# A two-layer kernel on one core: five buffers for weights, the index lookup by halves, gates that end five blocks earlier

## The chip, the core and the metric

One NeuronCore of a Trainium2 chip runs the whole program in one launch. The metric is device time in microseconds. Three runs of the kernel before took 2858.58, 2861.81 and 2862.98 us; the median is 2861.81.

TensorE (PE in the profile) multiplies matrices, VectorE (DVE) and ScalarE (ACT) work elementwise, GpSimd (POOL) issues the indirect gathers, and SyncE (SP) issues most of the other transfers. ACT issues some too.

## The reference

Two layers are computed on one sequence of 1024-wide tokens. Each layer is a mixer (A: gated linear attention and attention to a memory; B: stick-breaking attention) and a PEER step, each closed by a residual and a layer norm. PEER is where most of the time goes:

```
q        = x @ wq                              # 8 heads, two half queries each
s1, s2   = scores of the half queries against two sets of 128 subkeys
top16 of s1, top16 of s2 -> 256 sums -> top16  # per head
expert   = 128 * i1 + i2                       # 16384 experts
g        = softmax(best 16 scores)
y[t]     = sum over heads, experts of  g * gelu(x[t] . u[expert]) * v[expert]
x        = layer_norm(ALPHA * x + y)
```

All products are wanted in nearly fp32 precision.

## The kernel before, in words

**Tokens.** The first token tile (128 tokens) and 16 side tokens go by gather: for each chosen expert, POOL fetches a row of `un` or `vt`, and DVE multiplies and sums it (`gr` L1156, `va` L1175). The other tokens, 368 per chunk, go densely: all 16384 rows of u are multiplied with x, the result goes through gelu and is multiplied with a matrix of gates that is zero where an expert isn't chosen, and then comes the product with v.

**Blocks.** A PEER step runs 16 query blocks, 128 u blocks and 128 v blocks. A block of u is a 512 KB tile `ur` of raw weights, loaded by SP (L82). ACT rounds it (`uh`, L97), DVE subtracts to get the rest (`ul`, L98), and PE makes 24 matmuls of 128x368: eight chunks times `uh`·`xhi` (L117), `uh`·`xlo` (L118) and `ul`·`xhi` (L119). A v block has `vr`, `vh`, `vl` and 18 matmuls of 512 columns (L285, L287, L289) that accumulate into `acc`. The raw tiles have RB = 4 buffers and the split ones 3. In iteration b of the u loop the split of block b + 2 is made, so `ul` of block b + 2 stands on DVE behind all that iteration b puts there.

**Side work.** The same loop carries DVE's other work in small pieces, as Python generators that yield an estimate in ns. `work(...)` runs the top-k, the index lookup, the softmax and `gate_prep` of the next token tiles up to a budget per block (WB = 1000 once a tile is ready, WB0 = 1700 ahead of that). `gst(GR)` builds one-hots (`ob` L1462, `ob`·`gT` L1468, side tokens L1438) and has PE multiply them into gates (`pg` L1511), GR = 1.25 steps per block; `gus` handles the gathered rows with a budget of GU = 1230, and GU2 = 1350 or GU3 = 1900 once `work` is empty. The engines take their instructions in the order in which this program issues them.

**Index lookup** (L1283 to L1302). For four heads at a time, the 16 places in two lists are turned into indices: ACT spreads the list (`tb`), DVE compares the places with 0 to 15 (`eq` L1292, 128x1024), multiplies (L1296) and adds up in four steps (L1300, L1302). The two lists ("halves") have buffers of their own and go side by side, operation by operation.

**Gates.** ACT writes the gates to DRAM (`Gd`, L1516). When the last are written, SP loads the gates of the first v blocks into a tile that the profile calls `keep` (L1665, `keep<-Gd`), and ACT's queue issues the next two loads (`gl`). For a v block DVE and ACT multiply gates with activations into `w` (L1700, L1702), and ACT and DVE split it (`whi` L1704, `wlo` L1705).

**End of a PEER step.** The last TAIL = 5 v blocks are done tile by tile for each 128 tokens, and after each tile comes its layer norm (`lny` L984, `lnst` L985, and so on to L1001) while PE is at the next tile. After the last tile nothing covers the layer norm but the next mixer, or nothing at all at the end of the kernel.

Of the kernel before, what the change touches and what calls it, by code (L numbers as in the profile page):

```python
# [408 lines left out]
def mixer_a(E, a):  # L409
# [4 lines left out]
    with tc.tile_pool(name="acat", bufs=1, reuse_waits="tile") as ap:  # L414
# [11 lines left out]
        with psum_pool(E, acc=4, ps=4), tc.tile_pool(name="mixwk", bufs=2, reuse_waits="tile") as wk, \  # L426
# [4 lines left out]
            w2 = mp.tile([16, 3, P], F32, name="w2")  # L431
# [184 lines left out]
            with tc.manual_schedule(engines={mybir.EngineType.PE}):  # L616
# [8 lines left out]
                aT = [mp.tile([P, NT, P], F32, name=f"aT{h}") for h in range(GH)]  # L625
# [348 lines left out]
def layer_norm(E, lp, t, halves, gam, bet, hooks=()):  # L974
# [3 lines left out]
    y = lp.tile([P, D], F32, tag="lny", name="lny")  # L978
# [54 lines left out]
WB, WB0 = 1000, 1700  # L1033
# [7 lines left out]
GU2 = 1350  # L1041
GU3 = 1900
# [10 lines left out]
def peer(E, mixer, wq, sk, ut, vt, un, lng, lnb, out_dram=None, follow=()):  # L1053
# [10 lines left out]
    with ExitStack() as pp:  # L1064
# [118 lines left out]
        with ExitStack() as up:  # L1183
# [21 lines left out]
            class Sel:  # L1205
# [48 lines left out]
                def indices(self, h0=0, h1=8):  # L1254
# [28 lines left out]
                    for h in range(0, h1 - h0, ih):  # L1283
                        hs = slice(h, h + ih)
                        tb, eq = [], []
                        for half in range(2):
                            tb.append(wk.tile([P, 4, 16, 16], F16, tag=f"tb{half}", name="tb", bufs=1)[:, :ih])
                            nc.scalar.activation(tb[half], tv[:, half, hs, :, None].to_broadcast([P, ih, 16, 16]), AF.Copy)
                        for half in range(2):
                            eq.append(wk.tile([P, 4, 16, 16], F16, tag=f"eq{half}", name="eq", bufs=1)[:, :ih])  # L1290
                            av = ab[:, half, :n].rearrange("p (h k) -> p h k", k=16)
                            nc.vector.tensor_tensor(eq[half], av[:, hs, None, :].to_broadcast([P, ih, 16, 16]),  # L1292
                                                    E.iota16[:, None].to_broadcast([P, ih, 16, 16]), op=ALU.is_equal)
                        yield 300 * ih
                        for half in range(2):
                            nc.vector.tensor_mul(eq[half], eq[half], tb[half])  # L1296
                        yield 300 * ih
                        for m in (8, 4, 2):
                            for e in eq:
                                nc.vector.tensor_add(e[:, :, 0:m], e[:, :, 0:m], e[:, :, m:2 * m])  # L1300
                        for half, e in enumerate(eq):
                            nc.vector.tensor_add(self.i12[:, half, h0 + h:h0 + h + ih], e[:, :, 0], e[:, :, 1])  # L1302
                        yield 500 * ih
# [535 lines left out]
```

## Time and profile before

| | |
|---|---|
| median of three runs | 2861.81 us |
| the profiled execution, its own time | 2858.78 us |
| its span | 2857.1 us |
| PE busy | 2829.1 us |
| DVE busy | 2410.4 us |
| ACT busy | 1445.3 us |
| POOL busy | 778.2 us |
| mean DMA rate | 282 GB/s |

In the profiled execution layer 1's u blocks run from 335.65 to 901 us and its v blocks to about 1410 us; layer 2's u blocks run from 1754.47 to 2319.8 us. Rows of the timeline give start and duration in us, engine, line of the kernel, operation and tiles; in brackets stands how long the engine had been idle just before, and what ended that. A row with x2 or more has several instructions together.

### The profile page before, as it was taken

The numbers are of one execution on the slowest core, as the hardware profiler recorded it, in microseconds if no ns is written. First come the engines' busy times: TensorE is split into PE (matmuls) and PEld (weight loads), VectorE is DVE, ScalarE is ACT, GpSimd is POOL, SyncE is SP. The second block draws the span as 40 slices with busy tenths as digits, with TensorE's granted clock in tenths as the row PEclk, the third lists the DMA queues.
The fourth block names the chain that finished last, engine by engine and source line by source line (L and its number), as shares of the span: only waits on it lengthen the run. The fifth ranks groups of instructions, "written<-read, shape, count | busy, mean of one in ns | idle before, by whom it ended". The sixth has DMA issues, their size and how long they took to land. (4 is left out here: it accounts for less than half of the span.)

```text
span 2857.1 us, 44575 instructions
## 1 busy us (share of the span) xinstructions
PE 2829.1 (99%) x16144; PEld 2507.4 (88%) x16144; DVE 2410.4 (84%) x4944; ACT 1445.3 (51%) x2723; POOL 778.2 (27%) x584
## 2 busy tenths in 40 slices
PE   9999999999999999999999999999999999999998
PEld 7888899999998888888877789999999988888886
DVE  5567999999877888888868779999998778888888
ACT  6342446757674333433446424477676744334333
POOL 0100253333333333333000002433333333234330
PEclk9999999999999999999999999999999999999999
DMA  5332589989999999999521325989999999999994
GB/s 194 103 112 67 176 313 321 343 316 342 340 344 369 338 371 370 373 380 365 195 81 52 111 82 202 327 319 325 327 343 342 340 368 336 373 375 371 368 359 165
DMA packets 311070, 806.87 MB, mean 282 GB/s; under 512 B 32176, under 2 KB 124480, under 8 KB 304448
## 3 DMA queue, kind: packets, MB, share of 16 engines
q1 hardware_dynamic: 195936, 414.93, 42.0%
q0 software_dynamic: 78336, 285.25, 27.6%
q10 hardware_dynamic: 36576, 103.85, 9.5%
q8 instruction: 126, 2.06, 0.3%
q14 instruction: 96, 0.79, 0.1%
HBM read 708.19 MB, written 94.68 MB: 281 GB/s over the span
## 5 line engine op out<-in xcount | busy, mean ns | idle before, releaser
L117 PE MATMUL ph<-xhi,uh 128*128 128x368 f32 x2048 | 687.7, 336 | 0.0
L119 PE MATMUL ph<-xhi,ul 128*128 128x368 f32 x2048 | 674.0, 329 | 1.2 <-DVE ul L98 1.2
L118 PE MATMUL ph<-xlo,uh 128*128 128x368 f32 x2048 | 673.4, 329 | 0.0
L1103 POOL DMA_INDIRECT gr<-in_un,gidx x256 | 392.8, 1534 | 796.9 <-DVE gr L1156 595.3
L97 ACT ACTIVATE vh<-vr 128x1024 fp32r<-128x1024 f32 x256 | 271.3, 1060 | 497.7 <-PE acc L289 445.2
L1103 POOL DMA_INDIRECT gr<-in_vt,gidx x256 | 311.8, 1218 | 646.9 <-DVE va L1175 553.4
L285 PE MATMUL acc<-vh,whi 128*128 128x512 f32 x1536 | 474.5, 390 | 4.5 <-ACT whi L1704 4.5
L287 PE MATMUL acc<-vl,whi 128*128 128x512 f32 x1536 | 474.2, 390 | 0.2
L289 PE MATMUL acc<-vh,wlo 128*128 128x512 f32 x1536 | 473.6, 389 | 0.0
L98 DVE TENSOR_TENSOR vl<-vr,vh 128x1024 fp32r<-128x1024 f32 x256 | 313.5, 1225 | 160.1 <-ACT vh L97 156.6
L97 ACT ACTIVATE uh<-ur 128x1024 fp32r<-128x1024 f32 x288 | 304.1, 1056 | 197.9 <-PE ph L118 174.3
L119 PEld LDWEIGHTS ph<-xhi,ul 128*128 128x128 f32 x2048 | 384.7, 188 | 2.2 <-DVE ul L98 2.2
L118 PEld LDWEIGHTS ph<-xlo,uh 128*128 128x128 f32 x2048 | 385.4, 188 | 0.0
L117 PEld LDWEIGHTS ph<-xhi,uh 128*128 128x128 f32 x2048 | 385.1, 188 | 0.1
L98 DVE TENSOR_TENSOR ul<-ur,uh 128x1024 fp32r<-128x1024 f32 x288 | 351.1, 1220 | 34.3 <-ACT uh L97 34.3
L285 PEld LDWEIGHTS acc<-vh,whi 128*128 128x128 f32 x1536 | 287.9, 188 | 66.4 <-ACT whi L1704 7.0
L287 PEld LDWEIGHTS acc<-vl,whi 128*128 128x128 f32 x1536 | 288.3, 188 | 61.7 <-DVE vl L98 2.2
L289 PEld LDWEIGHTS acc<-vh,wlo 128*128 128x128 f32 x1536 | 288.2, 188 | 60.8 <-DVE wlo L1705 1.0
L1156 DVE SCALAR_TENSOR_TENSOR gr<-gr,xnat 128x1024 f32<-128x1024 f32 x256 | 310.3, 1218 | 24.5 <-DMA gr<-in_un,gidx 24.5
L1175 DVE SCALAR_TENSOR_TENSOR va<-gr,gw,va 128x1024 f32<-128x1024 f32 x254 | 325.2, 1281 | 1.0
L1491 ACT ACTIVATE obl<-ob,rat 128x128 f16<-128x128 f16 x736 | 234.1, 392 | 38.0 <-DVE ob L1468 18.3
L1704 ACT ACTIVATE whi<-w 128x384 fp32r<-128x384 f32 x256 | 131.1, 512 | 78.5 <-DVE w L1700 78.1
(358 smaller groups left out, 4091.4 us busy)
## 6 DMA issues: line engine op xcount, KB each, us to landing
ur<-in_ut SPq DMA_DIRECT2D x256, 512.0 KB
vr<-in_vt SPq DMA_DIRECT2D x256, 512.0 KB
Gd<-gt ACTq DMA_DIRECT2D x48, 1024.0 KB
Ad<-act ACTq DMA_DIRECT2D x112, 368.0 KB
al<-Ad SPq DMA_DIRECT2D x112, 368.0 KB
gl<-Gd SPq DMA_DIRECT2D x26, 1536.0 KB
ur<-in_wq SPq DMA_DIRECT2D x32, 512.0 KB
bs<-in_b_st SPq DMA_DIRECT2D x14, 512.0 KB
```

The source lines that it names most:

```text
L97: nc.scalar.activation(hi, raw, AF.Copy)
L98: sub = lambda: eng.tensor_sub(lo, raw, hi.bitcast(F32))
L117: nc.tensor.matmul(ps, h, xhi[:, c, sl], start=(c == 0), stop=False)
L118: nc.tensor.matmul(ps, h, xlo[:, c, sl], start=False, stop=False)
L119: nc.tensor.matmul(ps, l, xhi[:, c, sl], start=False, stop=(c == NC - 1))
L285: nc.tensor.matmul(acc[hf], lh, hi[:, hf * 512:(hf + 1) * 512], start=first, stop=False)
L287: nc.tensor.matmul(acc[hf], lh, lo[:, hf * 512:(hf + 1) * 512], start=False, stop=False)
L289: nc.tensor.matmul(acc[hf], ll, hi[:, hf * 512:(hf + 1) * 512], start=False, stop=last)
L1103: nc.gpsimd.indirect_dma_start(out=gr, out_offset=None, in_=tab, in_offset=bass.IndirectOffsetOnAxis(ap=idx[:, k:k + 1], axis=0))
L1156: nc.vector.scalar_tensor_tensor(gr, gr, 1.0, xr, op0=ALU.mult, op1=ALU.mult, accum_out=dst[:, k:k + 1])
L1175: nc.vector.scalar_tensor_tensor(va, gr, gw[:, k:k + 1], va, op0=ALU.mult, op1=ALU.add)
L1491: nc.scalar.activation(obl[:, q], ob[:, q, 0], AF.Copy, scale=rat[:, n0 + q:n0 + q + 1])
```

## The change

It has seven parts.

1. RB goes from 4 to 5; `w2` shares a buffer with `aT0`, `lny` has one buffer in place of two, and `tb` and `eq` have one each in place of two.
2. The index lookup goes half by half: all six operations of one half, then all of the other. ACT spreads the next half once DVE has multiplied the last one.
3. WB0 goes from 1700 to 1850; GU2 and GU3 become 1550 both; the gate builder makes 1.4 steps per block (GR2) once the `work` queue is empty; `work` falls to its small budget also where side gates are ready and more than one builder waits.
4. `gate_prep` yields after `ghi` and is told as 1000 + 1900 in place of 2500; the stream of the tiles yields 2000 in place of 4000 before the last one.
5. The gates end five blocks earlier, so the first load of gates and the first `w` move from the turn into the u blocks; the third load of gates is issued at v block 6 in place of 1.
6. The activation that loads the square-root table comes 8 v blocks later.
7. The last dense tile's tail runs by halves of 512 columns: first all 15 matmuls of the first half, then those of the second.

```diff
-WB, WB0 = 1000, 1700
+WB, WB0 = 1000, 1850
-GU2 = 1350
-GU3 = 1900
+GU2 = 1550
+GU3 = 1550
+GR2 = 1.4
-RB = 4
+RB = 5
...
-                    for h in range(0, h1 - h0, ih):
...
-                        yield 300 * ih
-                        for half in range(2):
-                            nc.vector.tensor_mul(eq[half], eq[half], tb[half])
-                        yield 300 * ih
-                        for m in (8, 4, 2):
-                            for e in eq:
-                                nc.vector.tensor_add(e[:, :, 0:m], e[:, :, 0:m], e[:, :, m:2 * m])
-                        for half, e in enumerate(eq):
-                            nc.vector.tensor_add(self.i12[:, half, h0 + h:h0 + h + ih], e[:, :, 0], e[:, :, 1])
-                        yield 500 * ih
+                    tb = spread(*todo[0])
+                    for k, (h, half) in enumerate(todo):
+                        eq = wk.tile([P, 4, 16, 16], F16, tag="eq", name="eq", bufs=1)[:, :ih]
...
+                        yield 150 * ih
+                        nc.vector.tensor_mul(eq, eq, tb)
+                        if k + 1 < len(todo):
+                            tb = spread(*todo[k + 1])
                         for m in (8, 4, 2):
+                            nc.vector.tensor_add(eq[:, :, 0:m], eq[:, :, 0:m], eq[:, :, m:2 * m])
+                        nc.vector.tensor_add(self.i12[:, half, h0 + h:h0 + h + ih], eq[:, :, 0], eq[:, :, 1])
+                        yield 400 * ih
...
                     nc.vector.tensor_copy(ghi, h16)
+                    yield 1000
...
-                    yield 2500
+                    yield 1900
...
-                yield 4000
+                yield 2000
                 yield from prev.gate_prep()
...
-                gst(GR)
+                gst(GR if work.q else GR2)
...
-                    work(WB if ready else WB0)
+                    work(WB if ready or sready and len(gst.q) > 1 else WB0)
...
-                if b == 1:
+                if b == 6:
                     preload(2)
...
                 if b == P // 2:
                     vp["ln"] = load_ln(E, wv, lng, lnb)
+                if b == P // 2 + 8:
                     warm_sqrt(E, vp["ln"][0])
...
+                if t < ND - 1:
+                    for k, (whi, wlo, hi, lo) in enumerate(tail):
+                        mov_mm(E, acc[t], whi[:, sl], wlo[:, sl], hi, lo, False, k == TAIL - 1)
+                else:
+                    for hf in range(2):
+                        hs = slice(hf * 512, (hf + 1) * 512)
+                        for k, (whi, wlo, hi, lo) in enumerate(tail):
+                            nc.tensor.matmul(acc[t][hf], whi[:, sl], hi[:, hs], start=False, stop=False)
+                            nc.tensor.matmul(acc[t][hf], whi[:, sl], lo[:, hs], start=False, stop=False)
+                            nc.tensor.matmul(acc[t][hf], wlo[:, sl], hi[:, hs], start=False, stop=k == TAIL - 1)
```

DVE's order before at u blocks 7 to 9 of layer 1, from the comparison behind `ul` of block 6 to `ul` of block 9 (`gr` is the product with a gathered row):

```order
L1292 TENSOR_TENSOR eq<-ab,iota_65 128x1024 x2
L1156 SCALAR_TENSOR_TENSOR gr,gh<-gr,xnat 128x1024
L98 TENSOR_TENSOR ul<-ur,uh 128x1024
L1296 TENSOR_TENSOR eq<-eq,tb 128x1024 x2
L1156 SCALAR_TENSOR_TENSOR gr,gh<-gr,xnat 128x1024
L98 TENSOR_TENSOR ul<-ur,uh 128x1024
L1300 TENSOR_TENSOR eq<-eq 128x4x128 x2
L1300 TENSOR_TENSOR eq<-eq 128x4x64 x2
L1300 TENSOR_TENSOR eq<-eq 128x4x32 x2
L1302 TENSOR_TENSOR i_2258<-eq 128x64 x2
L1156 SCALAR_TENSOR_TENSOR gr,gh<-gr,xnat 128x1024
L98 TENSOR_TENSOR ul<-ur,uh 128x1024
```

And in the changed kernel, the block of the first half, from the comparison to `ul` of block 7:

```order
L1295 TENSOR_TENSOR eq<-ab,iota_65 128x1024
L1298 TENSOR_TENSOR eq<-eq,tb 128x1024
L1302 TENSOR_TENSOR eq<-eq 128x4x128
L1302 TENSOR_TENSOR eq<-eq 128x4x64
L1302 TENSOR_TENSOR eq<-eq 128x4x32
L1303 TENSOR_TENSOR i_2258<-eq 128x64
L1157 SCALAR_TENSOR_TENSOR gr,gh<-gr,xnat 128x1024
L98 TENSOR_TENSOR ul<-ur,uh 128x1024
```

The pair took three blocks, each operation twice in a row; a half takes one block with all its six operations, and the other half follows in the next block in the same way.

At the turn from u to v, DVE's order before, from the gathered rows at the last `ul` of layer 1 (the first `w` belongs to v block 0):

```order
L98 TENSOR_TENSOR ul<-ur,uh 128x1024
L1156 SCALAR_TENSOR_TENSOR gr,gh<-gr,xnat 128x1024 x3
L1700 TENSOR_TENSOR w<-keep 128x368
L98 TENSOR_TENSOR vl<-vr,vh 128x1024
L1705 TENSOR_TENSOR wlo<-w,whi 128x384
```

And in the changed kernel, from the first `w` on:

```order
L1702 TENSOR_TENSOR w<-keep 128x368
L98 TENSOR_TENSOR ul<-ur,uh 128x1024
L1157 SCALAR_TENSOR_TENSOR gr,gh<-gr,xnat 128x1024 x2
L98 TENSOR_TENSOR ul<-ur,uh 128x1024
L1157 SCALAR_TENSOR_TENSOR gr,gh<-gr,xnat 128x1024
L98 TENSOR_TENSOR ul<-ur,uh 128x1024
L1157 SCALAR_TENSOR_TENSOR gr,gh<-gr,xnat 128x1024
L98 TENSOR_TENSOR ul<-ur,uh 128x1024
L1157 SCALAR_TENSOR_TENSOR gr,gh<-gr,xnat 128x1024
L98 TENSOR_TENSOR ul<-ur,uh 128x1024
```

The first `w` stood behind the last `ul`; now six `ul` (the sixth stands two rows further on) come after it. SP's order at the same turn, before, from the last loads of u:

```order
L82 DMA ur<-in_ut 128x1024 x77
L1665 DMA keep<-Gd 128x24x96
L82 DMA vr<-in_vt 128x1024 x4
L1695 DMA al<-Ad 128x736
L82 DMA vr<-in_vt 128x1024
```

And in the changed kernel:

```order
L82 DMA ur<-in_ut 128x1024 x74
L1667 DMA keep<-Gd 128x24x96
L82 DMA ur<-in_ut 128x1024 x4
L1697 DMA al<-Ad 128x736 x2
L82 DMA vr<-in_vt 128x1024
```

The load of the first gates, which waits for the last of them to be written, now stands before the last four loads of u in place of behind them all.

More of the change, by code (lines that the diff above doesn't have):

```diff
@@ L430, in mixer_a @@
             kv1 = [mp.tile([P, 2, 256], F32, name=f"kv1{k}") for k in range(2)]
-            w2 = mp.tile([16, 3, P], F32, name="w2")
+            w2 = mp.tile([16, 3, P], F32, tag="aT0", name="w2")
             gl = mp.tile([P, NT, 16], F32, name="gl")
@@ L624, in mixer_a @@
                     pass
-                aT = [mp.tile([P, NT, P], F32, name=f"aT{h}") for h in range(GH)]
+                aT = [mp.tile([P, NT, P], F32, tag=f"aT{h}", name=f"aT{h}") for h in range(GH)]
                 for t_ in aT:
@@ L977, in layer_norm @@
     nc = E.nc
-    y = lp.tile([P, D], F32, tag="lny", name="lny")
+    y = lp.tile([P, D], F32, tag="lny", name="lny", bufs=1)
     st = E.lnp.tile([P, 2, 6], F32, tag="lnst", name="lnst", bufs=2)
@@ L1282, in indices @@
                     tv = tif.rearrange("p (h two) k -> p two h k", two=2)
-                    for h in range(0, h1 - h0, ih):
-                        hs = slice(h, h + ih)
-                        tb, eq = [], []
-                        for half in range(2):
[L1287 to L1293, printed above, removed]
-                        yield 300 * ih
-                        for half in range(2):
-                            nc.vector.tensor_mul(eq[half], eq[half], tb[half])
-                        yield 300 * ih
-                        for m in (8, 4, 2):
-                            for e in eq:
-                                nc.vector.tensor_add(e[:, :, 0:m], e[:, :, 0:m], e[:, :, m:2 * m])
-                        for half, e in enumerate(eq):
-                            nc.vector.tensor_add(self.i12[:, half, h0 + h:h0 + h + ih], e[:, :, 0], e[:, :, 1])
-                        yield 500 * ih
@@ L1745, in peer @@
                 sl = slice(t * P, (t + 1) * P)
-                for k, (whi, wlo, hi, lo) in enumerate(tail):
-                    mov_mm(E, acc[t], whi[:, sl], wlo[:, sl], hi, lo, False, k == TAIL - 1)
+                if t < ND - 1:
[8 more added lines that the diff above has]
+                            nc.tensor.matmul(acc[t][hf], wlo[:, sl], hi[:, hs], start=False, stop=k == TAIL - 1)
                 if last:
```

8 lines of the change are left out of this document (added).

## The prediction

> **What bounds the kernel now.** I read the page's first table, then PE's waits, then the windows of the u phase, and then the timeline at the places where PE stood.
>
> ```profile
> PE 2829.1 (99%) x16144; PEld 2507.4 (88%) x16144; DVE 2410.4 (84%) x4944; ACT 1445.3 (51%) x2723; POOL 778.2 (27%) x584
> ...
> PE vga L491 <- ACT xhi L463: 4.8, 1, 4.8
> PE acc L285 <- ACT whi L1704: 4.5, 5, 2.5
> PE bsp L133 <- DVE bsl L98: 1.6, 2, 1.1
> PE pg L1446 <- DVE ob L1438: 1.6, 2, 0.8
> PE ph L119 <- DVE ul L98: 1.2, 2, 0.6
> ```
>
> PE is busy 2829.1 of a 2857.1 us span, so all its waits come to 28 us, 1% of the time. The change adds and removes no matmul. It can win only out of those 28 us, and it loses wherever it makes another engine late for PE. So the sum is a ledger of PE's waits: which go, and which come.
>
> The engine that can be late in the u phase is DVE:
>
> ```profile
> 420.00:680.00 260.00, 258.63 (x1820) 251.62 (x1818) 249.35 (x655) 175.00 (x374) 94.93 (x59) 1.00 0.92 327
> 680.00:905.00 225.00, 224.51 (x1559) 218.01 (x1559) 186.96 (x294) 154.77 (x334) 86.43 (x61) 1.00 0.96 350
> 345.27:406.02 60.75, 60.75 (x366) 60.75 (x365) 59.40 (x172) 29.95 (x39) 25.55 (x16) 1.00 0.87 311
> ```
>
> The columns are length, then busy time of PE, PEld, DVE, ACT and POOL, granted clock, DMA share, GB/s. In layer 1's u phase DVE is busy 96% up to 680 us, 83% after it, and 98% in the first 15 blocks (last row). PE's clock is 1.00, so a block has a fixed price. DVE has no room early and has room late.
>
> **The index lookup by halves: a dearer chain on DVE.** Rows of the operations, grouped by form for 420 to 905 us, then one lookup in order of time:
>
> ```profile
> L1296 DVE TENSOR_TENSOR eq<-eq,tb 128x1024 f16<-128x1024 f16 x8 | 5.2, 686 | 0.8 <-ACT tb L1288 0.8
> L1292 DVE TENSOR_TENSOR eq<-ab,iota 128x1024 f16<-128x1024 f16 x8 | 5.1, 685 | 0.0
> L1300 DVE TENSOR_TENSOR eq<-eq 128x512 f16<-128x512 f16 x8 | 3.0, 419 | 0.0
> L1300 DVE TENSOR_TENSOR eq<-eq 128x256 f16<-128x256 f16 x8 | 2.0, 286 | 0.0
> L1300 DVE TENSOR_TENSOR eq<-eq 128x128 f16<-128x128 f16 x8 | 1.4, 219 | 0.0
> ```
> ```profile
> 393.86 1.29 DVE L1292 TENSOR_TENSOR eq<-ab,iota 128x1024 f16<-128x1024 f16 x2
> 395.06 1.29 DVE L1296 TENSOR_TENSOR eq<-eq,tb 128x1024 f16<-128x1024 f16 x2
> 396.27 1.22 DVE L1156 SCALAR_TENSOR_TENSOR gr<-gr,xnat 128x1024 f32<-128x1024 f32 x1
> ...
> 398.55 1.43 DVE L1300 TENSOR_TENSOR eq<-eq 128x512 f16<-128x512 f16 x6
> 399.89 0.35 DVE L1302 TENSOR_TENSOR i<-eq 128x64 f32<-128x64 f16 x2
> 400.17 1.22 DVE L1156 SCALAR_TENSOR_TENSOR gr<-gr,xnat 128x1024 f32<-128x1024 f32 x1
> ...
> 459.48 1.22 DVE L1462 TENSOR_TENSOR ob<-iota,iT 128x2048 f16<-128x2048 f16 x1
> 460.73 0.69 DVE L1468 TENSOR_TENSOR ob<-ob,gT 128x1024 f16<-128x1024 f16 x1
> ```
>
> Two comparisons of 0.685 us each start 0.60 us apart (393.86 to 395.06 is 1.20 for two), because the two halves don't need each other and overlap at their ends. Where the next operation reads what the last one wrote, it waits for the end: L1468 starts 460.73 − 459.48 = 1.25 us after L1462, whose own duration is 1.22, so 0.03 is added instead of something being saved. A pair of halves now costs (396.27 − 393.86) + (400.17 − 398.55) = 2.41 + 1.62 = 4.03 us, 2.02 per half. In the changed order all six operations of a half are one chain: five at their own duration plus 0.03, 0.685 + 0.686 + 0.419 + 0.286 + 0.219 + 0.15 = 2.45, and the last, which the next may overlap, at 0.14 (half of 400.17 − 399.89). That is 2.58 us, **0.57 dearer per half**. The budget is told 2200 ns for it. There are 32 halves in the kernel.
>
> On this the Trainium skill speaks the other way: "VectorE: DVE Perf Modes", section "The DRAIN you can't avoid", says that after each operation the next doesn't start until the pipe is empty, so that a wait between two of them costs nothing extra. By that rule halves would cost what pairs cost, and the loss below would shrink as in the first rival. The rows disagree: 0.60 us from start to start where 0.685 is one's duration.
>
> **What that does in blocks 4 to 18.** The `ul` of block b must be done when PE reaches its third matmul.
>
> ```profile
> 344.05 1.21 DVE L98 TENSOR_TENSOR ul<-ur,uh 128x1024 fp32r<-128x1024 f32 x1
> ...
> 348.07 0.33 PE L119 MATMUL ph<-xhi,ul 128*128 128x368 f32 x1
> ...
> 408.07 0.33 PE L119 MATMUL ph<-xhi,ul 128*128 128x368 f32 x1
> ```
>
> These are the `ul` of block 3, which ends at 345.27 where the window above begins, the matmul that needs it, and the same matmul of block 18, whose `ul` ends where the window ends. Block 3 has 348.07 − 345.27 = 2.80 us to spare; PE takes 60.0 us for the 15 blocks, DVE 60.75, of which 59.40 busy. In the new order, the same 15 stretches from `ul` to `ul` hold six whole halves where two pairs and one pair's comparisons stood. The dearer chains are 6 × 0.57 = 3.4 us, and the rest of the third pair (4.03 − 1.20 = 2.8) is drawn in by WB0 1850; smaller shifts take 0.1 off: 6.1 us more. Another pair lies ahead of block 0, which costs 2 × 0.57 less a comparison pulled forward, some 1.0, so block 3 has 1.8 us spare. PE must then wait for 60.75 + 6.1 − 60.0 − 1.8 = 5.0 us if DVE's idle 1.35 stays, and 3.7 if it vanishes. I take 4.4 per layer, in pieces of 0.1 to 0.9 at blocks 7, 8, 11 to 13, 17 and 18.
>
> **Blocks 51 to 53.** Spare time isn't piled up without limit: a one-hot waits for PE to finish the gates of two before.
>
> ```profile
> DVE ob L1462 <- PE pg L1511: 43.4, 24, 4.9
> ...
> 491.31 1.22 DVE L98 TENSOR_TENSOR ul<-ur,uh 128x1024 fp32r<-128x1024 f32 x1
> ...
> 494.52 0.33 PE L119 MATMUL ph<-xhi,ul 128*128 128x368 f32 x1
> ```
>
> After such a wait `ul` ends at 492.53, 2.0 us before its matmul. In the new order blocks 46 and 48 have such one-hots, and blocks 51 to 53 list 6.6, 5.1 and 5.4 us (summed like the half above, from the rows of the same operations), 17.1 together; PE's three steps are 4.0 us and, where gates stand between, 4.5, some 13.0. 17.1 − 13.0 − 2.0 = 2.1 us of waiting; another tenth or two at block 89. I take 2.2 per layer. New waits in the u phases: 2 × (4.4 + 2.2) = **+13.2**.
>
> **What goes in the u phase.** Gate preparation is cut in two, and side work stands elsewhere, so the two stalls of each layer lose their cause:
>
> ```profile
> 590.21 0.44 PE L119 MATMUL ph<-xhi,ul 128*128 128x368 f32 x1 [0.58 <-DVE ul L98]
> 594.95 0.23 PE L1446 MATMUL pg<-ob 128*128 128x128 bf16 x1 [0.80 <-DVE ob L1438]
> ```
>
> By the rows of PE's waits for both layers, 1.2 + 1.6: **−2.8**. Blocks 56 to 62 list less than PE takes on the whole, and nothing is late next.
>
> **The turn from u to v.**
>
> ```profile
> 901.24 0.73 PE L285 MATMUL acc<-vh,whi 128*128 128x512 f32 x2 [0.37 <-ACT whi L1704]
> 908.11 9.38 ACTq L1665 DMA_DIRECT2D gl<-Gd  x1
> ...
> 2319.97 1.23 DVE L1156 SCALAR_TENSOR_TENSOR gr<-gr,xnat 128x1024 f32<-128x1024 f32 x1 [1.76 <-DMA gr<-in_un,gidx]
> 2321.12 0.54 DVE L1700 TENSOR_TENSOR w<-keep 128x368 f32<-128x368 f32 x1
> 2322.32 0.50 PE L285 MATMUL acc<-vh,whi 128*128 128x512 f32 x1 [2.53 <-ACT whi L1704]
> ```
>
> In layer 2 the first weights `w` stand on DVE behind a gather that is late by 1.76 us, and PE waits 2.53; in layer 1 0.37. In the new order `w` comes before the `ul` of block 122, so both go. At 908.11 ACT's queue is held for 9.38 us by the second load of gates, behind which the `whi` of block 7 is late: the rest of PE's wait for `whi`, 4.5 − 2.53 − 0.37 = 1.6, holds that and small ones. Issued at b = 6 the load finds the first one landed, and it is used at b = 14 at the earliest. I count 0.9 of the 1.6, and leave 0.2 for the turn itself: 2.53 + 0.37 + 0.9 − 0.2 = **−3.6**. The fifth buffer, which lets `vr` loads start a block sooner, is part of that and nothing beside it: no row of PE or DVE names `ur`.
>
> **The last tile by halves.**
>
> ```profile
> 2847.39 1.28 DVE lny L984 x2
> 2848.68 1.21 DVE lnst L985 x2
> ```
>
> From the chain that ended last: both halves' sums, then both halves' statistics, after the last matmul. The first half's (0.64 + 0.60) now lie beside the other half's 15 matmuls of 0.23 us: **−1.2** at the end. Ahead of mixer B the same 1.2 us starts work that PE waits for (`bsp` 1.6 in its waits, and small ones); other work is on that path, and I count **−0.9**, between 0 and 1.2. Everything else (the shared tags, one `lny`, the moved square-root load) I put at nothing, covered by PE's own work; uncovered, each is under 0.5.
>
> **Sum.** 13.2 − 2.8 − 3.6 − 1.2 − 0.9 = +4.7. The profiled execution took 2858.8 us (1.7 around its span), 3.0 below the median of the runs, 2861.8; all terms are against the profiled one: **2863.5 us**. A measurement of this kernel tells about 0.2% or 5.7 us from no change, so this counts as the same.
>
> **Rivals.**
>
> *Halves cost what pairs cost.* Then the first stretch loses 3.4 of its 4.4 and the second two halves' 1.1: new waits 2 × (1.0 + 1.1) = 4.2, and the change is 4.2 − 8.5 = −4.3: 2854.5. For it: the rule above. Against it: the overlapping rows. 15%.
>
> *DVE's lists don't bind at all*, because spare time ahead of block 0 is larger than 1.8 and blocks 46 to 53 are spread better than I read: −8.5, 2850.3. For it: before, only 2.8 us of waits came out of lists as full as 98%. Against it: 6.1 us are added in a window with 1.35 idle. 22%.
>
> *The first gates come late for the u blocks.* They are loaded once the last gates are written:
>
> ```profile
> 2296.40 0.33 ACTq L1516 DMA_DIRECT2D Gd<-gt  x1
> 2304.55 0.38 SPq L1665 DMA_DIRECT2D keep<-Gd  x1
> 2316.81 0.22 ACT L1702 ACTIVATE w<-keep 128x16 f32<-128x16 f32 x1 [7.73 <-DMA keep<-Gd]
> ```
>
> Write 8.2 us, load 12.3 us. Now DVE's `w` stands before the `ul` of block 122, with five more `ul` behind it, ACT's `w` before five `uh`, and SP's load before the last four `ur`. By the new order the last gates end PE's block 115, and as at 2296.40 the write follows about 1.6 us behind, 2.4 ahead of block 117; 20.4 us later, 2.0 us into block 121, `w` can start. `ul` of 122 is due 4.3 us into it, and `w` and `ul` take 0.54 and 1.14: 0.7 us to spare. From there on each us of delay is a us of PE. If the load takes a quarter longer (3.1 us), PE loses 2.4 per layer: 2863.5 + 4.8 = 2868.3. For it: the DMA share there is 0.96. Against it: both layers took the same within 1.5 us. 18%, and where it comes beside the forecast's stalls the time is slower.
>
> **How the numbers follow.** The forecast (+1 to +8) has 42%, some 33 of it within 0.2% and 9 above; the first rival 15% (11 same, 4 faster); the second 22% (20 faster, 2 same); late gates 18% (16 slower, 2 same); 3% are left. So faster 0.25, same 0.48, slower 0.27. The range runs from the second rival's 2850 to 2870, beyond the third's; the forecast's own is 2860 to 2867.
>
> **What would show it.** Right: PE's waits name `ul` L98 many times, 10 us and more in all, at blocks 7 to 18 and 51 to 53 of each layer; a half's operations lie 2.6 us from first to last; PE's wait for `whi` falls under 1 us; `lny` after the last matmul is single. Wrong: PE waits for `ul` under 4 us (then DVE had more room), or a gap before block 122 whose chain goes to `keep<-Gd` (then the third rival), or PE waits for `uh` because the single `tb` holds ACT's next spread until DVE's multiplication.

## The result, and the profile after

The changed kernel is slower: 2875.62 us, the median of 5 runs (2874.74 to 2877.66), where the kernel before took 2859.56 beside it (5 runs). The ratio is 1.0052, with a 95% interval of 1.0040 to 1.0064. The forecast was 2863.5 us, with a range of 2850 to 2870.

The page's first table after, then the longest rows of PE's waits (us in total, how often, longest):

```profile
PE 2836.2 (99%) x16144; PEld 2514.1 (87%) x16144; DVE 2425.6 (84%) x4944; ACT 1440.8 (50%) x2723; POOL 767.0 (27%) x584
```
```profile
PE ph L119 <- DVE ul L98: 8.8, 15, 0.9
PE vga L491 <- ACT xhi L463: 5.4, 1, 5.4
PE pg L1513 <- ACT obl L1493: 5.1, 2, 2.5
PE bsp L117 <- DVE lny L984: 4.1, 1, 4.1
PE bsp L133 <- DVE bsl L98: 1.8, 1, 1.8
PE gtp L1342 <- DVE best L1315: 0.7, 2, 0.4
PE acc L285 <- ACT whi L1706: 0.7, 2, 0.3
```

Three of these rows hold most of the loss: the wait for `ul`, which was forecast, and those for `obl` and `lny`, which no part of the prediction names. `whi` has fallen from 4.5 to 0.7, as forecast. And PE is busy 7.1 us longer with the same 16144 matmuls. Some 5.1 of that is time in which its clock was halved, as will be seen; the rest was not followed.

To place the time, the starts of the first and last matmuls of each stage were read from both timelines. The profiled spans are 2857.1 and 2873.6 us, +16.5.

| stage | before, us | after, us | change | forecast |
|---|---|---|---|---|
| start to u, layer 1 | 0 to 335.65 | 0 to 334.91 | −0.74 | 0 |
| u, layer 1 | to 900.54 | to 909.32 | +9.52 | +5.2 |
| turn | to 901.24 | to 909.49 | −0.53 | with v |
| v, layer 1 | to 1428.31 | to 1434.39 | −2.17 | with v |
| layer norm, mixer B, queries | to 1754.47 | to 1765.12 | +4.57 | −0.9 |
| u, layer 2 | to 2319.46 | to 2340.76 | +10.65 | +5.2 |
| turn | to 2322.32 | to 2340.93 | −2.69 | with v |
| v, layer 2 | to 2847.19 | to 2864.08 | −1.72 | turns and v: −3.6 |
| last matmul to the end | to 2857.1 | to 2873.6 | −0.39 | −1.2 |

The sum is +16.5 in place of +4.7. The u phases and mixer B are too dear, the turns better than forecast, and the end gives nearly nothing.

**The u phase, block by block.** The third matmul of each block (the first with `ul`, L119) was read from both timelines, and the shift after minus before counted from block 0. It grows by 6.0 us in blocks 4 to 20, by 4.6 at blocks 49 and 50 and by 1.1 at blocks 89 to 91, and falls by 2.2 where the two stalls of before stood; 9.5 is left. (Gates that fall into other blocks shift it for a while and are given back. They were taken out by the same curve of the run `best` below, which has none of the new stalls.) Layer 2 has the same curve within 0.1 us up to block 120, and then 1.1 more.

*Blocks 4 to 20.* DVE's rows for one half, and PE's behind it (bracket: idle time and what ended it):

```profile
364.99 0.69 DVE L1295 TENSOR_TENSOR eq<-ab,iota 128x1024 f16<-128x1024 f16 x1
365.71 0.69 DVE L1298 TENSOR_TENSOR eq<-eq,tb 128x1024 f16<-128x1024 f16 x1
366.44 1.01 DVE L1302 TENSOR_TENSOR eq<-eq 128x512 f16<-128x512 f16 x3
367.48 0.23 DVE L1303 TENSOR_TENSOR i<-eq 128x64 f32<-128x64 f16 x1
367.62 1.22 DVE L1157 SCALAR_TENSOR_TENSOR gr<-gr,xnat 128x1024 f32<-128x1024 f32 x1
368.77 1.22 DVE L98 TENSOR_TENSOR ul<-ur,uh 128x1024 fp32r<-128x1024 f32 x1
...
370.04 0.44 PE L119 MATMUL ph<-xhi,ul 128*128 128x368 f32 x1 [0.65 <-DVE ul L98]
```

A half takes 367.62 − 364.99 = 2.63 us, forecast 2.58. With `gr` and `ul` at 1.14 us each from start to start, such a block is 4.9 us on DVE, while PE needs 4.0.

The stretch from the `ul` of block 3 to that of block 18, 60.75 us long with 59.40 of DVE busy before, is now this (length, then PE, PEld, DVE, ACT, POOL busy, clock, DMA share, GB/s):

```profile
345.84:413.19 67.35, 63.67 (x370) 61.06 (x369) 64.96 (x183) 29.55 (x38) 25.54 (x16) 1.00 0.80 281
```

*Block 49.* A stall the prediction did not list, here in layer 1. PE is between its blocks 48 and 49; the prediction and the expectations speak of blocks 51 to 53 and of block 51 here.

```profile
549.61 0.69 DVE L1298 TENSOR_TENSOR eq<-eq,tb 128x1024 f16<-128x1024 f16 x1
...
550.40 1.06 ACT L1288 ACTIVATE tb<-tif 128x1024 f16<-128x1024 f16 x1 [0.96 <-DVE eq L1298]
...
551.36 1.04 ACT L97 ACTIVATE uh<-ur 128x1024 fp32r<-128x1024 f32 x1
...
552.30 0.46 ACT L1630 ACTIVATE act<-ph 128x368 f32<-128x368 f32 x1
...
553.16 0.60 ACT L1516 ACTIVATE gt<-pg 128x512 f32<-128x512 f32 x1 [0.40 <-ACT act L1630]
553.66 1.26 ACT L1493 ACTIVATE obl<-ob,rat 128x128 f16<-128x128 f16 x4
...
554.11 0.23 PE L1513 MATMUL pg<-ob,obl 128*128 128x128 f16 x1 [2.54 <-ACT obl L1493]
```

Read from the end: PE waits 2.54 us for ACT's `obl`. In front of it on ACT stand `gt`, `act`, `uh` and the spread `tb`, and `tb` had waited 0.96 us for DVE's multiplication, because `tb` has one buffer. A late DVE so makes ACT late, and ACT makes PE late at a place where `ul` is in time.

**PE's clock.** Windows of after, around three of its long waits (columns as above; the clock is the third number from the end):

```profile
551.28:554.69 3.41, 0.85 (x11) 0.34 (x7) 3.34 (x7) 3.01 (x8) 1.67 (x1) 1.00 0.83 324
554.69:558.10 3.41, 3.41 (x13) 3.25 (x14) 3.20 (x10) 3.02 (x6) 0.17 (x2) 0.50 0.87 319
1435.33:1438.74 3.41, 0.00 (x0) 0.00 (x0) 3.32 (x5) 0.00 (x0) 1.76 (x6) 1.00 0.44 154
1438.74:1442.15 3.41, 3.29 (x15) 3.32 (x16) 3.15 (x10) 0.20 (x1) 0.00 (x0) 0.50 0.00 0
1448.98:1452.39 3.41, 1.65 (x14) 1.45 (x13) 2.42 (x3) 0.69 (x2) 0.00 (x0) 1.00 0.14 55
1452.39:1455.80 3.41, 3.41 (x19) 3.41 (x18) 0.00 (x0) 0.00 (x0) 0.00 (x0) 0.50 0.41 159
```

After each of these waits PE runs 3.41 us at clock 0.50, which loses 1.7 us of work on top of the wait. After has four such stretches ahead of its end (554.69, 1438.74, 1452.39, and 1984.87 in layer 2). Before has one, behind the wait at the turn of layer 2:

```profile
2319.34:2322.75 3.41, 0.88 (x5) 0.44 (x3) 2.78 (x5) 1.56 (x4) 1.07 (x2) 1.00 1.03 411
2322.75:2326.16 3.41, 3.41 (x10) 2.64 (x9) 3.36 (x7) 3.20 (x7) 0.00 (x0) 0.50 1.03 406
```

Three stretches more, at 1.7 us, are 5.1 of the 16.5 us.

**Mixer B.** PE's first matmul of the stage (`bsp`) and the last one of v, with DVE's second `lny` of the last tile, after:

```profile
1434.39 0.40 PE L1758 MATMUL acc<-vh,wlo 128*128 128x512 f32 x1
...
1438.05 0.67 DVE L984 SCALAR_TENSOR_TENSOR lny<-xnat,acc 128x512 f32<-128x512 f32 x1
...
1438.86 0.55 PE L117 MATMUL bsp<-xhi,bsh 128*128 128x256 f32 x1 [4.08 <-DVE lny L984]
```

and before:

```profile
1428.07 0.63 PE L289 MATMUL acc<-vh,wlo 128*128 128x512 f32 x2
...
1428.54 0.28 PE L117 MATMUL bsp<-xhi,bsh 128*128 128x256 f32 x1
...
1429.49 0.68 DVE L984 SCALAR_TENSOR_TENSOR lny<-xnat,acc 128x512 f32<-128x512 f32 x1
```

Before, `bsp` began while the last tile's `lny` was still to come. After, it waits for that `lny`, 4.08 us, though it uses nothing of it. What it needs is the place: `bsp` gets a bank of PSUM that `acc` has left. In the compiled programs the banks of `acc` go by the order of first use in v block 0. `bsp`'s first bank was that of the middle tile's `acc`, read long ago; now it is that of the last tile's second half, which is read last of all. The runs below agree: in the five kernels where `bsp`'s first bank is the last tile's (the change, rb4, rb4_pairs, rb4_twotb, tail_last) PE waits 3.2 to 4.3 us for `lny` there, and in the seven others, where it is the middle tile's, the first `bsp` doesn't wait.

**The turn of layer 2 and the late first gates.** After, no wait stands between the last `ph` and the first `acc`, and in layer 2 there is one earlier, at block 122:

```profile
2315.42 0.54 DVE L1702 TENSOR_TENSOR w<-keep 128x368 f32<-128x368 f32 x1 [8.16 <-DMA keep<-Gd]
...
2317.15 0.44 PE L119 MATMUL ph<-xhi,ul 128*128 128x368 f32 x1 [0.89 <-DVE ul L98]
...
2340.76 0.33 PE L119 MATMUL ph<-xhi,ul 128*128 128x368 f32 x1
2340.93 0.62 PE L285 MATMUL acc<-vh,whi 128*128 128x512 f32 x2
```

The load, issued at 2303.93, lands some 11.5 us later, `w` holds DVE for it, and `ul` behind `w` costs PE 0.89 us, and 1.1 in the curve of the blocks. Layer 1 shows none in this execution.

**The end.**

```profile
2862.37 1.42 DVE L1001 SCALAR_TENSOR_TENSOR xnat<-lny,lnsm,bet 128x512 f32<-128x512 f32 x2
2863.90 1.30 DVE L984 SCALAR_TENSOR_TENSOR lny<-xnat,acc 128x512 f32<-128x512 f32 x2
...
2864.08 0.40 PE L1758 MATMUL acc<-vh,wlo 128*128 128x512 f32 x1
```

`lny` still appears as x2 behind the tile before. The first half was ready 3.5 us before PE's end (15 matmuls of 0.23), but DVE finished the layer norm of the tile before only at 2863.8.

### The profile page after: what moved, and what is told of

Same layout as the page of the kernel before. It is cut to its first block, busy times and chain, and to the rows that moved or that the text cites. A ratio compares the mean times of both kernels' runs of the same rounds, so it can differ in the third digit from the quotient of the medians.

```text
span 2873.6 us, 44638 instructions
## 1 busy us (share of the span) xinstructions
PE 2836.2 (99%) x16144; PEld 2514.1 (87%) x16144; DVE 2425.6 (84%) x4944; ACT 1440.8 (50%) x2723; POOL 767.0 (27%) x584
## 4 chain that ended last, share of the span: by engine, by line
PE 39%; DVE 8%; DMA 1%; ACT 1%; issue 1%; DVEq 0%; ACTq 0%
PE acc L285 6%; PE acc L287 6%; PE acc L289 6%; PE ph L117 4%; PE ph L119 4%; PE ph L118 4%; DVE ul L98 2%; DVE gr L1157 1%; PE bsp L117 1%; PE bsp L119 1%; PE bsp L118 1%; PE pg L1512 1%; PE pg L1513 1%; PE oacc L285 1%; PE oacc L289 1%
## 5 line engine op out<-in xcount | busy, mean ns | idle before, releaser
L119 PE MATMUL ph<-xhi,ul 128*128 128x368 f32 x2048 | 677.1, 331 | 9.0 <-DVE ul L98 8.8
L1104 POOL DMA_INDIRECT gr<-in_un,gidx x256 | 400.0, 1562 | 821.9 <-DVE gr L1157 601.6
L1104 POOL DMA_INDIRECT gr<-in_vt,gidx x256 | 289.3, 1130 | 672.1 <-DVE va L1176 593.2
L285 PE MATMUL acc<-vh,whi 128*128 128x512 f32 x1516 | 467.2, 389 | 0.7 <-ACT whi L1706 0.7
L287 PE MATMUL acc<-vl,whi 128*128 128x512 f32 x1516 | 467.0, 389 | 0.0
L289 PE MATMUL acc<-vh,wlo 128*128 128x512 f32 x1516 | 466.9, 389 | 0.0
L119 PEld LDWEIGHTS ph<-xhi,ul 128*128 128x128 f32 x2048 | 385.5, 188 | 15.3 <-DVE ul L98 15.0
L1516 ACT ACTIVATE gt<-pg 128x512 f32<-128x512 f32 x184 | 109.3, 594 | 89.3 <-PE pg L1513 61.5
```

The lines of the kernel that those rows point to most:

```text
L119: nc.tensor.matmul(ps, l, xhi[:, c, sl], start=False, stop=(c == NC - 1))
L285: nc.tensor.matmul(acc[hf], lh, hi[:, hf * 512:(hf + 1) * 512], start=first, stop=False)
L287: nc.tensor.matmul(acc[hf], lh, lo[:, hf * 512:(hf + 1) * 512], start=False, stop=False)
L289: nc.tensor.matmul(acc[hf], ll, hi[:, hf * 512:(hf + 1) * 512], start=False, stop=last)
L1104: nc.gpsimd.indirect_dma_start(out=gr, out_offset=None, in_=tab, in_offset=bass.IndirectOffsetOnAxis(ap=idx[:, k:k + 1], axis=0))
```

## The experiments

The first theory was that three things of the change lose time: the lookup by halves together with its larger budget, the single `tb`, and the end by halves ahead of mixer B; and that the fifth buffer and the moved gates don't. Each run undoes or does one of these. Times are medians; the kernel before ran beside each group (2861.07, 2860.82 and 2860.31 us), and the ratio to it is the comparison's own, with its 95% interval.

| run | edit (to the changed kernel, unless said) | us | ratio | u 1, u 2 | mixer B |
|---|---|---|---|---|---|
| the change itself | | 2875.62 | 1.0052 [1.0040, 1.0064] | +9.5, +10.7 | +4.6 |
| rb4 | four buffers | 2877.93 | 1.0057 [1.0041, 1.0074] | +9.5, +9.5 | +7.2 |
| rb4_twotb | four buffers, two `tb` | 2874.94 | 1.0052 [1.0034, 1.0070] | +6.9, +8.2 | +6.7 |
| rb4_pairs | four buffers, lookup by pairs | 2858.61 | 0.9994 [0.9984, 1.0003] | +0.7, +0.4 | +5.0 |
| wb0 | WB0 1700 | 2854.98 | 0.9982 [0.9973, 0.9991] | +1.9, +2.0 | −0.2 |
| told | halves told at their price | 2856.23 | 0.9992 [0.9982, 1.0001] | +4.1, +2.0 | −0.6 |
| tail_last | halves at the kernel's end only | 2872.76 | 1.0036 [1.0022, 1.0051] | +9.5, +10.2 | +2.2 |
| bank | v block 0 in another order | 2871.73 | 1.0042 [1.0026, 1.0057] | +10.7, +9.5 | −0.5 |
| turn_alone | before, with the turn's edits | 2856.70 | 0.9988 [0.9979, 0.9997] | −0.2, −0.3 | 0.0 |
| best | see below | 2848.09 | 0.9959 [0.9945, 0.9972] | −1.7, −1.6 | −0.1 |
| best_both | best, halves in both layers | 2851.46 | 0.9968 [0.9956, 0.9980] | −2.2, −2.3 | +1.5 |

The last two columns are steps of the profiled executions against that of before. Some of the u steps hold late first gates: waits of 0.3 to 2.4 us, in one layer or both, that differ from run to run.

**rb4: the fifth buffer alone.** It is also the control for the next two, since with five buffers neither pairs nor two `tb` fit in the on-chip memory.

```diff
-RB = 5
+RB = 4
```

> The changed kernel with four raw buffers in place of five; everything else as changed. Theory: the fifth buffer has no part in the loss, and little in the gain at the turn from u to v. Then the waits of PE in the u blocks stay as they are in the changed kernel (ul 8.8 us in 15 waits, obl 5.1 us in 2), and the whole is within 2 us of it, about 2874 to 2878 us. Rival: the fifth buffer is what makes the turn smooth; then PE's waits at the two turns come back (0.4 and 2.5 us and the blocked queue behind them), the v phases lose the 2 us each that they gained, and the whole is 2879 us or more.

The fifth buffer takes waits away. ACT's waits before, with four buffers:

```profile
ACT vh L97 <- DMA vr<-in_vt: 52.5, 21, 5.9
```

and in rb4:

```profile
ACT vh L97 <- DMA vr<-in_vt: 92.3, 31, 6.9
```

With five there is no such row. PE hardly feels it in the v phases: those of rb4 gain 1.7 us each all the same, against 2.2 and 1.7 with five. But PE feels the fifth buffer in the mixers, whose output weights `wo` are loaded into the same raw buffers and split into `woh` and `wol`. In rb4 two of its waits there are these, and with five neither row is there:

```profile
PE oacc L285 <- ACT woh L97: 1.1, 1, 1.1
...
PE oacc L287 <- DVE wol L98: 0.5, 1, 0.5
```

From the first to the last matmul of `oacc`, the kernel before takes 47.9 us in layer 1 and 46.8 in layer 2. All five kernels with five buffers take 46.3 to 46.4 and 45.2, and all seven with four take 47.1 to 48.9 and 46.0 to 47.5. So the fifth buffer gains 1.6 us in each mixer against the kernel before, 3.1 in all, which the prediction put at nothing. The whole is as expected, but rb4's step of +7.2 in mixer B, against +4.6, holds the lost gain.

**rb4_pairs: the lookup by pairs, all else as changed.**

```diff
+RB = 4
-for k, (h, half) in enumerate(todo): ...     # one half at a time
+for h in range(0, h1 - h0, ih): ...          # the two lists side by side, as before
```

> As the run with four buffers, but with the index lookup by pairs as before (both halves side by side, two buffers each for the comparison and the spread list); the budget WB0 stays at 1850. Theory of the dearer chain: 16 halves per layer cost 0.57 us less on DVE, and the spare time ahead of block 0 is 1.0 us larger, so that the waits for ul in blocks 4 to 18 go nearly all (6.0 us per layer to 0.5 or less), and those at blocks 51 to 53 and at block 90 too; both u phases together get 18 to 21 us shorter, and the whole is 2855 to 2858 us. Rival, the budget: WB0 1850 draws 2.8 us of work forward into the first 18 blocks whatever the form of the lookup; then half of the 6.0 us stay and the whole is 2862 to 2867 us.

The u phases fall from +9.5 to +0.7 and +0.4, and the whole to that of before. PE's row for `ul`, of which 1.3 and 1.0 are late first gates, one in each layer:

```profile
PE ph L119 <- DVE ul L98: 3.1, 4, 1.3
```

So the lookup's form is the cause of nearly all of the u phases' loss at this budget. In blocks 4 to 20, 1.5 us are left, more than expected, and the whole is 0.6 us above its expectation.

**rb4_twotb: the coupling of ACT and DVE.**

```diff
-tb = wk.tile([P, 4, 16, 16], F16, tag="tb", ...)
+tb = wk.tile([P, 4, 16, 16], F16, tag=f"tb{half}", ...)
-tb = spread(*todo[0])
+tbs = [spread(*todo[0]), spread(*todo[1])]
...
-if k + 1 < len(todo): tb = spread(*todo[k + 1])
+if k + 2 < len(todo): tbs.append(spread(*todo[k + 2]))
```

> As the run with four buffers, by halves, but with two buffers for the spread list, both filled ahead, so that ACT's next spread waits for the half before last. Theory of ACT's queue: at block 51 ACT stands behind the spread, which waits for DVE's multiplication, and uh, the gates and obl come late behind it; then the 4.7 us per layer there (2.7 of waiting for obl and slow matmuls after it) fall to what DVE's own lateness gives, 2 us or less, while the waits for ul in blocks 4 to 18 stay at 6 us; the whole is 2869 to 2872 us. Rival: DVE's lateness alone sets both; then nothing changes, 2874 to 2878 us.

PE's wait for `obl` falls from 5.1 to 1.1 us, while that for `ul` rises:

```profile
PE ph L119 <- DVE ul L98: 10.1, 17, 1.1
...
PE pg L1514 <- ACT obl L1494: 1.1, 2, 0.5
```

No stretch at clock 0.50 follows block 49 any more, and what the place costs falls from 4.6 to 2.1 us in layer 1. The 2.1 is the size that was forecast for DVE's list, but only 0.9 of it is a wait for `ul`, at block 53; the other 1.2 still stand at block 49, behind ACT's `obl`. Layer 2 holds 1.4 us of late gates. The whole came out higher than expected: mixer B stayed dear, with four buffers more so.

**wb0 and told: the budget.** The first takes the old budget with the dear halves, the second the new budget with yields that tell a half's true price (645 × 4 = 2580 ns).

```diff
-WB, WB0 = 1000, 1850
+WB, WB0 = 1000, 1700
```

> The changed kernel (lookup by halves) with WB0 1700 in place of 1850 and all else as changed. Theory: the dearer chain and the larger budget each take spare time, and stalls come where the sum runs out; summed list by list as in the prediction, blocks 4 to 22 lose about 1.6 us per layer in place of 4.0 (measured 6.0 with 1850), and blocks 51 to 57 about 0.5 in place of 2.2 (measured 4.7): the u phases get 12 to 17 us shorter together, and the whole is 2859 to 2864 us. Rival, the chain alone: the halves' six dependent operations are late whatever the budget; then less than a third goes, and the whole is 2870 us or more.

```diff
-yield 150 * ih
+yield 176 * ih
...
-yield 400 * ih
+yield 469 * ih
```

> The changed kernel with one thing changed: the lookup's yields say what a half takes by the changed trace, 2580 ns in place of 2200 (176 and 469 per head in place of 150 and 400); WB0 stays at 1850, the operations and their order within a half stay. Theory: a block can take budget times (true over told), plus 2.28 us for its gather and its ul, and PE has 4.01. By halves at 1850 that is 1.85 x 2.58 / 2.20 + 2.28 = 4.45, at 1700 4.27, by pairs at 1850 (4.40 told, 4.03 true) 3.97; told truly it is 4.13. So the u phases lie between those of the run with WB0 1700 (1.9 and 2.0 us more than before) and of the pairs at 1850 (0.7 and 0.4 more); the banks are right in this order; the whole is 2852 to 2856 us. Rival, the form of the chain: six dependent operations in one block are late whatever they are told to take; then the u phases keep 6 us or more per layer, and the whole is 2865 us or more.

wb0 came out some 4 us under its expectation and told at the edge of its own; wb0 is faster than before by more than its interval. In wb0 the u phases got 16.2 us shorter, as expected; mixer B, 4.8 us shorter than in the change for another reason (below), makes up the rest. No wait for `obl` is left in either. With `rb4_pairs` and `best` they make a table of the loss in layer 1, from the curves of the blocks:

| lookup, budget | DVE per block, us | blocks 4 to 20 | blocks 49 to 62 |
|---|---|---|---|
| halves, 1850 (the change) | 1.85 × 2.63 / 2.20 + 2.28 = 4.5 | 6.0 | 4.6 |
| halves, 1700 (wb0) | 4.3 | 3.5 | 0.6 |
| halves told right, 1850 (told) | 4.2 | 3.6 | 0.2 |
| pairs, 1850 (rb4_pairs) | 1.85 × 4.03 / 4.40 + 2.28 = 4.0 | 1.5 | 0 |
| pairs, 1700 (best) | 3.8 | 0 | 0 |

The second column is the budget times what a lookup takes over what it is told, and 2.28 for `gr` and `ul`; PE's block takes 4.0. The loss follows it. The dear halves alone lose 4.1, the larger budget alone 1.5, and the two together 10.6, with DVE half a us per block over PE and, at block 49, ACT and the clock drawn in. Told its true price at the larger budget, the lookup by halves still loses 3.8, against 1.5 by pairs.

**tail_last and bank: mixer B.** The first theory was that halves in layer 1 hold the buffers of the split tiles longer, so that ACT's `bsh` comes late (it does: the first starts 2.3 us ahead of the start of the last v matmul in place of 5.1).

```diff
-if t < ND - 1:
+if t < ND - 1 or not last:
```

> The changed kernel with the last tile by halves only at the end of the kernel, and in layer 1 as before. Theory: by halves the five split tiles of the last v blocks are held until the second half has used them, so that the split of mixer B's first weights, which takes their buffers, and DVE's queue behind it come late, and the first matmuls of mixer B wait 4.1 us; as before, they start at once. Then the way from the end of layer 1's v blocks to the queries of layer 2 gets 4 to 5 us shorter (227.2 us to 222.6), and the whole is 2870 to 2872 us. Rival: the single buffer for lny holds DVE there, which stays; then the gain is under 1.5 us.

```profile
PE bsp L117 <- DVE lny L984: 3.2, 1, 3.2
```

Half a miss: the step fell from +4.6 to +2.2, but most of the wait for `lny` stayed, 3.2 of 4.1 us; 1.7 of the 2.4 go with the second stretch at clock 0.50, which is gone here. So the halves are not the main cause of the wait, and the bank was tried, by the order in which `acc` is first used:

```diff
-for t in (0, 2, 1):
+for t in ((0, 1, 2) if b == 0 else (0, 2, 1)):
```

> The changed kernel, but v block 0 alone runs its tiles in the order 0, 1, 2 in place of 0, 2, 1, so that the PSUM banks that mixer B's first matmuls take are those of the middle tile, and not of the last tile's second half. Theory of the bank: PE's 4.1 us wait for lny at the head of mixer B goes whole, and with it the slow matmuls behind it; the layer norm on DVE is late by about 1 us still, so that the way from the end of layer 1's v blocks to the queries of layer 2 falls from 227.2 us to 223.5 to 224.5 (222.6 before); the whole is 2871.5 to 2873 us. Rival: DVE's late queue (the split of mixer B's first weights, which waits for tiles that the halves hold longer) sets it; then PE waits the 4 us at the next place, and the whole stays at 2874 to 2878 us.

```profile
1435.41 0.39 PE L1758 MATMUL acc<-vh,wlo 128*128 128x512 f32 x1
1435.64 0.28 PE L117 MATMUL bsp<-xhi,bsh 128*128 128x256 f32 x1
```

The wait is gone, with both stretches at clock 0.50 behind it, and the step is −0.5 in place of +4.6, more than expected. Up to the first `oacc` the stage is 1.0 us longer than before, as the theory had it: PE now waits 1.7 us for DVE's `xlo` (`xtp`, L966), where it waited 0.5 before. The fifth buffer's 1.6 at `oacc` makes up for that. In wb0 the step is −0.2 with the order unchanged: there `bsp` got the middle tile's bank anyhow. The assignment moves with edits that have nothing to do with it.

**turn_alone: the part that wins, on the kernel before.**

```diff
+GR2 = 1.4
-GU2 = 1350
-GU3 = 1900
+GU2 = 1550
+GU3 = 1550
-gst(GR)
+gst(GR if work.q else GR2)
...
-if b == 1:
+if b == 6:
                     preload(2)
```

> The kernel before with one part of the change: the gates' last steps at 1.4, the gather budgets 1550 both, the third load of gates at v block 6; lookup by pairs, four buffers, WB0 1700, the last tile as before. The gates end three blocks earlier and the first w stands before the ul of block 125. Theory: PE's waits at the turns and the blocked queue behind them go, 7 us of both layers as in the changed kernel, less 1.2 us per layer where the first gates come late for the ul behind w; mixer B and the u blocks as before: 2852 to 2856 us against 2859 to 2861. Rival: the turn's gain needs the gates five blocks earlier; then the waits for the first gates at the turn eat most of it, and the whole is within 2 us of before.

Faster by 0.12%, and 0.7 us above its expectation. The turns win 0.5 and 2.7 us as in the change, and the stretch at clock 0.50 at 2322.75 is gone. In the profiled execution, one of the longer ones of this run (2860.62 us), the v phases are 1.9 and 1.7 us longer than before, where ACT waits 113.9 us for `vr`. Why that is more than in rb4, which also has four buffers, stays open.

**best: what the runs point to.** Pairs, WB0 1700, four buffers, two `lny`, halves at the kernel's end only, and v block 0 in the order 2, 0, 1. The rest of the change stays: part 4, the condition for the small budget in part 3, the shared `w2` and part 6 were not tried alone.

> The changed kernel with the lookup by pairs, WB0 1700, four raw buffers and two lny, the last tile by halves only at the end of the kernel, and v block 0 in the order 2, 0, 1 for mixer B's banks. Theory: every loss is taken out and every gain kept. The u phases lose their old stalls too (about 2 us per layer), the turns gain 7 us less 1.2 per layer for late first gates, mixer B is as before, the end gains 0.4 to 1.0: 2849 to 2853 us. Rival: the parts share a cause that isn't found, and the whole is within 3 us of before, 2857 us or more.

```profile
PE ph L119 <- DVE ul L98: 0.6, 2, 0.4
...
PE xtp L966 <- DVE xlo L971: 0.5, 1, 0.5
```

It beats both kernels: 12.7 us under the median of before. Against before, its stages are −1.7 and −1.6 in the u phases, −0.5 and −2.7 at the turns, −2.2 and −1.8 in v, −0.1 in mixer B and −0.7 at the end. The last comes from the second `lny`: the first half's sums now start at 2834.23, amid the layer norm of the tile before, whose buffer they needn't wait for. It came out 0.9 us under its expectation, and its four buffers still cost it the waits for `woh` and `wol`.

**best_both** is the same with halves in layer 1 too.

```diff
-if t < ND - 1 or not last:
+if t < ND - 1:
```

> As the best run so far, with the last tile by halves in layer 1 as well. Theory: with the banks right, the halves cost nothing at the head of mixer B, and gain nothing either, since DVE's layer norm of the tile before takes as long as a tile's matmuls: 227.2 - 4.6 = 222.6 us from the end of layer 1's v blocks to the queries of layer 2, within 1 us, and the whole is 2847 to 2850 us. Rival: the split tiles held longer delay mixer B's first weights; then that way is 2 us or more longer.

Mixer B is 1.6 us dearer than in best, between the theory and the rival. In the profiled executions 1.0 of that is this wait, which is 0.5 us in best, and the rest stands at `oacc`:

```profile
PE xtp L966 <- DVE xlo L971: 1.6, 1, 1.6
```

The intervals of the two whole times overlap, and the whole lies 1.5 us above its expectation. Halves ahead of mixer B show no gain, and a loss of about 1 us where they are traced.

## Why the prediction was wrong

**The u blocks 4 to 18: right in kind and place, 1.6 us short per layer.** 4.4 was forecast, 6.0 measured up to block 20, in waits for `ul` as described. DVE's stretch was forecast at 60.75 + 6.1 = 66.85 us if its idle time stayed, and 1.35 less if that vanished; I took the middle. It was 67.35: busy time rose by 5.6, and idle time by 1.0, about what the gaps of 0.03 us within the chains come to. Of the 1.35 us nothing was given up. The time to spare at block 3 was 1.5 (347.33 − 345.84, by the timeline), forecast 1.8. So 67.35 − 60.0 − 1.5 = 5.9. The step that failed is the middle taken between idle time that stays and idle time that goes (0.6 us); the stretch was another 0.5 longer than the upper case, and the spare time 0.3 shorter.

**Blocks 51 to 53: 2.2 was forecast, 4.6 measured at blocks 49 and 50, and the wait named was the wrong one.** DVE's list made PE wait less than was said: rb4_twotb, which frees ACT in part, shows 0.9 us for `ul` at block 53. The prediction followed DVE alone and put the single buffer of `tb` at nothing; it has a line on it only among the things that would show it wrong, and for `uh`. ACT's queue carried DVE's lateness to `obl`, 2.54 us, and the halved clock took 1.7 more. Another 1.1 us per layer, from late halves at blocks 89 to 91 (`gtp` after `best` among them), was listed only as a tenth or two.

**Clock: the step that was missing.** The prediction writes that the clock is 1.00, so that a block has a fixed price, and counts a wait at its length. That nearly holds for the waits of under 1 us. A longer one can cost 1.7 us more. The Trainium skill has the rule ("TensorE: Matmul & The Clock Gate", section "What's actually happening": half speed after an idle window of some 3.4 us, on windows that run freely). The trace agrees on the windows, and differs on what counts as idle, as below. The trace of the kernel before shows such a stretch behind the wait at layer 2's turn, and the prediction should have priced that wait by it.

**The turns and v: −3.6 was forecast, −7.1 measured.** The mechanism was right: `w` ahead of `ul`, and no wait at the turn. Of the 3.5 us more, 1.7 are the halved clock behind the old wait at 2322.32; that is the whole gain of layer 2's v phase. Another 0.5 is at the turns themselves. The rest is in layer 1's first five v blocks, which took 22.55 us before and 20.41 after, 2.1 less where the prediction counted 0.9.

**Mixer B: this step failed, −0.9 forecast, +4.6 measured.** It assumed that layer norm work begun earlier lets PE begin earlier. PE's first matmul did not depend on that work at all; it depended on which bank it got. Up to the first `oacc` the stage is 6.15 us longer than before in the change and 1.04 in `bank`, with the same tail by halves: so the bank costs 5.1 us, the two stretches at clock 0.50 included. The 1.0 that is left goes with the halves, as best_both against best shows. They cost here where a gain was forecast.

**The fifth buffer: put at nothing beside the turns, and worth 3.1 us.** The prediction reasoned that no row of PE or DVE names `ur`. The raw buffers hold `wo` too, and PE's waits at `oacc` name `woh` and `wol`. This gain hides part of mixer B's loss: +6.15 up to the first `oacc`, and −1.6 from there on.

**The end: −1.2 was forecast, −0.4 measured.** The forecast laid the first half's sums beside the other half's matmuls without asking whether DVE is free then. It mostly isn't: a tile's layer norm fills 2857.39 to 2863.8, 6.4 of the 6.9 us that a tile's matmuls take (30 of 0.23). And the single `lny`, put at nothing, makes the sums wait for the end of that layer norm; with two, in best, they start amid it and the end gives −0.7.

**The rivals.** "Halves cost what pairs cost" fell: 2.63 us for a half, 2.02 in a pair. It leaned on the rule of the Trainium skill's "VectorE: DVE Perf Modes", "The DRAIN you can't avoid", that the next operation doesn't start until the pipe is empty. The traces show that only for the chain: operations that read what the last one wrote start 0.72 us apart (365.71 − 364.99), independent ones of the same 0.685 us 0.60. The same section of the Trainium skill says too that a next operation that isn't held starts earlier, which the prediction left out. "DVE's lists don't bind" fell with the 8.8 us of waits. "The first gates come late" came true beside the forecast, with 1.1 us in layer 2 here and a wait of 2.4 in one layer of `told`; its price of 2.4 per layer was the upper end. It had been given a chance as a rival where it was a term to add.

**The sum.** Added to +4.7: new u stalls +10.2 (2 × (6.0 + 4.6 + 1.1) = 23.4 in place of 13.2), old stalls −1.6 (4.4 gone in place of 2.8), late gates +1.1, mixer B +5.5, the end +0.8, turns and v −3.5, and the start −0.7. That is the +16.5. The start's −0.7 is the fifth buffer's −1.6 at `oacc`, against a first wait of the kernel that is 0.7 longer (5.4 in place of 4.8 us; it goes from 4.6 to 5.7 over the runs). Two terms outweigh the rest: the u stalls were sized at little over half, and mixer B had the wrong sign.

## What to carry to other kernels

A budget that is told a price must be told the true one, in the form in which the work will run: halves with a price 16% too low (2.20 for 2.63 us) and a budget 9% larger cost 4.1 and 1.5 us per layer apart, and 10.6 together. When a buffer is cut to one, follow the queue of the engine that fills it, not only of the one that reads it. When one is added, look for its readers in every stage that shares it. And when a stage begins with a matmul that waits for something it doesn't use, look at which PSUM bank it was given, and who read that bank last.

## What the runs showed of the hardware

The clock goes down after waits that are shorter than one window. The stretches at 0.50 in the changed kernel are each 3.41 us long up to its last matmul, and their starts lie whole multiples of 3.413 us apart (1452.39 − 1438.74 = 4 of them, 1438.74 − 554.69 = 259). In the window ahead PE was busy 0.00, 0.85, 0.86 and 1.65 us of 3.41, and 0.88 in the kernel before. A window with a little more is not followed by one. The first row is `bank`, around its wait for `xlo`; the other two are `told`, where PE waits 2.38 us for late gates, but across the border of two windows:

```profile
1442.12:1445.53 3.41, 1.73 (x15) 1.46 (x13) 3.23 (x10) 0.05 (x1) 0.00 (x0) 1.00 0.00 0
...
891.38:894.79 3.41, 1.97 (x12) 1.67 (x10) 0.80 (x2) 0.72 (x2) 0.00 (x0) 1.00 0.95 369
894.79:898.20 3.41, 2.48 (x15) 2.48 (x16) 3.41 (x6) 2.65 (x6) 1.12 (x1) 1.00 0.52 168
```

So in these runs the border lies between 1.65 and 1.73 us of work in a window, about half of it, and no window of the twelve traces that began at clock 1.00 contradicts it. The same wait costs its length or 1.7 us more, by where it falls. Once down, the clock needs more work than that to come back: in rb4_pairs a window at 0.50 with 2.47 us of work (from 1430.37) is followed by a second one at 0.50, so that its stretch is 6.83 us long.
